# Summing the shift and scale parts of a modulation block in one tile, with other shares for VectorE and TensorE, and low parts of the first weights on GpSimd

## The chip, the cores and the metric

The kernel runs on one core of a Trainium2 chip. The metric is device time in microseconds of one execution, lower is better; the time before is the median of three runs, 2203.69 us (2201.57 to 2204.17). A core has TensorE (PE in the profile, its weight loads apart as PEld), VectorE (DVE), ScalarE (ACT), GpSimd (POOL) and queues for transfers, most of which SyncE (SP) issues here.

## The reference, cut to what the change touches

```python
c_act = jax.nn.silu(c)                            # c: (1, 1024)
mod = c_act @ w_mod[l] + b_mod[l]                 # w_mod: (1024, 3072)
shift, scale, gate = jnp.split(mod, 3, axis=-1)
h = rms_norm(x, g_norm[l]) * (1.0 + scale[:, None, :]) + shift[:, None, :]
proj = h @ w_in[l]                                # x: (1, 2048, 1024), w_in: (1024, 8192)
...
```

The projection feeds a recurrent branch and an attention branch, which are merged, projected and added to x. All of that lies behind the part in question. Here it matters that `h` needs shift and scale for each of its 1024 channels before the first product, and that each of these is a sum over 1024 terms `c_act[k] * w_mod[k, m]`.

## The kernel before, in words

Channels are laid on the 128 partitions, so 1024 channels are eight groups k (`KT = 8`, `KH = 4` is half of them). The first bank of 512 positions is built group by group: four transposes on TensorE turn x into channels by positions (`turn_x`, L688, to `turned`, L554), ScalarE makes the high part of h from PSUM with gain `gs` and bias `sh` (L564) and once more the full value `hf` (L567), and VectorE subtracts the two for the low part (L168). High and low parts let TensorE multiply in a reduced format three times and add (`mm3`): 12 multiplications of 512 columns a group (`products(k)`, four outputs of three). Their other operand, the first eight rows of tiles of the value weights (`raws`), is split in the same way by `split_k`: high part on ScalarE (L159), low part by `lo_dve` on VectorE (L168).

Shift and scale come in four blocks j of 256 channels, that is, two groups each. Tile `w_m[j, q]` holds all eight k of block j for shift (q = 0) or scale (q = 1), 1 MB, loaded by SyncE (L649). A block's sum over k is shared between two engines. `KV[j][q]` says how many k VectorE takes (`sums`): the first with one instruction of 256 elements (L658), each further one with a multiply-add on an accumulator (L661). TensorE takes the others (`column_sums`): for each k two multiplications with one column, the weights as the stationary operand and `ca[:, k]` as the moving one, into a PSUM tile V. Then `last_sums` folds VectorE's accumulators over the partitions, by the same kind of multiplication with a column of ones, and `modulation` (L684, L685) adds the bias and makes the gain on VectorE. In the profile a one-column multiplication leaves two records each of a weight load and a multiplication.

`idle_matmuls` issues multiplications of 512 columns on constants (tile `busy`), whose results nobody reads; here they are called fillers. `column_sums(0, 0, fill=1)` puts one behind every second k.

All this stands inside `manual_schedule()`: each engine runs its instructions in the order of the program's text. From the loop over j on, the order is: last sums of block j, its modulation, the rest of the products of group 2j - 1, turn of group 2j + 1, build and products of group 2j, VectorE's terms of block j + 1, with build 2j + 1 among them, splits of the next weights, turn of group 2j + 2, column sums of block j + 1 and the first half of the products of group 2j + 1. So the modulation of block j + 1 comes behind all of VectorE's terms and TensorE's columns for it. Behind this part (from L802 on) a planner orders the instructions up to the attention, which has an order of its own.

x itself is normalised first: ScalarE sums squares of its four tiles of rows (L715), VectorE finishes the factor (L172 to L181) and scales rows 0, 1 and 3 (L718), ScalarE row 2 (L734).

Of the kernel before, what the change touches and what calls it, by code (L numbers as in the profile page):

```python
# [20 lines left out]
P = 128  # L21
# [21 lines left out]
KV = (0, 3), (4, 3), (6, 5), (6, 5)  # L43
# [47 lines left out]
def decoder_block(ctx, tc, x, c, positions, g_norm, w_mod, b_mod, w_in, b_gate, conv_w, conv_b,  # L91
# [551 lines left out]
    w_m, px, accs = {}, {}, {}  # L643

    def load_mod(j):
        for q in range(2):
            w_m[j, q] = t = T(hp, [P, KT, 256], F32, "T", bufs=14)
            c0 = q * D + j * 256
            nc.sync.dma_start(t[:], w_mod[0, :, c0 : c0 + 256].rearrange("(k p) m -> p k m", p=P))  # L649

    def sums(j, q, ks=range(KT)):

        t = w_m[j, q]
        for k in ks[: KV[j][q] - ks[0]]:
            c = ca[:, k : k + 1]
            if k == 0:
                accs[j, q] = T(vx, [P, 256], F32, "acc", bufs=4)
                nc.vector.tensor_scalar(accs[j, q][:], t[:, k, :], c, None, ALU.mult)  # L658
            else:
                acc = accs[j, q]  # L660
                nc.vector.scalar_tensor_tensor(acc[:], t[:, k, :], c, acc[:], ALU.mult, ALU.add)  # L661

    def column_sums(j, q, fill=0):
        if q == 0:
            px["mod"] = T(pj, [P, 2, 2], F32, "V")
        pm, t = px["mod"], w_m.pop((j, q))
        for k in range(KV[j][q], KT):
            for i in range(2):
                mm(pm[:, q, i : i + 1], t[:, k, i * P : (i + 1) * P], ca[:, k : k + 1],
                   q == i == 0 and k == KV[j][0], q == i == 1 and (j, q) not in accs and k == KT - 1, skip_group_check=True)  # L670
            if fill and k % 2:
                idle_matmuls(fill)

    def last_sums(j, q):
        if (j, q) in accs:
            acc = accs.pop((j, q))
            for i in range(2):
                mm(px["mod"][:, q, i : i + 1], acc[:, i * P : (i + 1) * P], ones[:, 0:1],
                   False, q == i == 1, skip_group_check=True)
# [14 lines left out]
    with tc.manual_schedule():  # L694
# [21 lines left out]

        def scale_dve(r):
            nc.vector.tensor_scalar(x0[r], x0[r], norm[r // 2][:, 1, r % 2 : r % 2 + 1], None, ALU.mult)  # L718
# [11 lines left out]
        scale_dve(0)  # L730
        scale_dve(1)
        rstd_first(norm[1])
        rstd_last(norm[1])
        nc.scalar.activation(x0[2], x0[2], AF.Copy, scale=norm[1][:, 1, 0:1])  # L734
# [7 lines left out]
        def split_k(k):  # L742
            split_wide(ws[k // KH], k, raws.pop(k), lo_dve)
            n = k + NRAW
            if n < KT + KH:
                raws[n] = load_wide_raw(n // KT, n % KT)

        idle_matmuls(6)
        column_sums(0, 0, fill=1)
        idle_matmuls(2)  # L750
        sums(0, 1)
        column_sums(0, 1)
        split_k(0)
        idle_matmuls(2)
        last_sums(0, 1)
        modulation(0)
        turn_x(0)
        build_x(0)
        turn_x(1)
        idle_matmuls(2)  # L760
        split_k(1)
        pv0 = [pj_tile([P, CH]) for j in range(KH)]
        products(0)
        sums(1, 0)
        build_x(1)
# [5 lines left out]
        column_sums(1, 1)  # L771
        x1 = load_x(hp, 1, "T", 14)
        for j in range(1, 4):
            k = 2 * j
            for q in range(2):
                last_sums(j, q)
            modulation(j)
            products(k - 1, (2, 3))
            if j == 1:
                split_k(3)  # L780
# [3 lines left out]
            if j < 3:  # L784
                sums(j + 1, 0, range(3))
            build_x(k + 1)
            if j < 3:
                sums(j + 1, 0, range(3, KT))
                split_k(k + 2)
                turn_x(k + 2)  # L790
                column_sums(j + 1, 0)
                products(k + 1, (0, 1))
                sums(j + 1, 1)
                column_sums(j + 1, 1)
                split_k(k + 3)
# [1364 lines left out]
```

## Time and profile before

| | |
|---|---|
| median of three runs | 2203.69 us |
| the profiled execution | 2198.89 us |
| its span, first to last instruction | 2197.1 us |
| granted TensorE clock, mean over the span | 0.994 |
| the stretch up to 63 us: TensorE busy, granted clock | 58.73 us, 0.89 |
| the same: VectorE, ScalarE, GpSimd busy | 31.23, 26.47, 4.45 us |

Each row of a timeline has start and duration in us, engine, line, operation, tile written and tiles read with their sizes, the count of merged instructions and, in brackets, the engine's idle time before it and what ended it. In a row of windows each engine has its busy time and, in brackets, its count of instructions; then follow the granted TensorE clock (1.00 is full speed), the share of time that the 16 DMA engines were busy, and GB/s. In a row by line or tile, the three durations are the least, the median and the greatest in ns. Busy times of TensorE come from pipelined instructions that overlap, so the step from one to the next is shorter than the duration of one.

### The profile page before, as it was taken

How to read it: one execution, taken by the hardware profiler on the slowest of the kernel's cores; microseconds unless marked ns; L12 is line 12 of the kernel's file. 1: busy time of each engine (PE TensorE's matmuls, PEld its weight loads, DVE VectorE, ACT ScalarE, POOL GpSimd, SP SyncE). 2: the span in 40 equal slices, each digit the busy share in tenths (PEclk: the TensorE clock that was granted, in tenths of full speed). 3: DMA queues.
4: the chain of work that ended last, by engine and by line, in shares of the span. 5: the costliest groups of instructions: out<-in, count | busy, mean ns of one | idle time of the engine just before them, and what ended most of it. 6: DMA issues, size and time to landing. Idle time of an engine off the chain costs nothing.

```text
span 2197.1 us, 32892 instructions
## 1 busy us (share of the span) xinstructions
PE 2158.3 (98%) x10633; PEld 1804.7 (82%) x10634; DVE 1475.3 (67%) x2569; ACT 1311.0 (60%) x2619; POOL 1076.5 (49%) x804
## 2 busy tenths in 40 slices
PE   9999999999999999999999999999999999999998
PEld 7878888887788888888888887888888988877886
DVE  4748888867656715545447574566777777688887
ACT  3747678667644627457547522677888887434333
POOL 0457677766666423223224665465666665200443
PEclk8999999999999999999999999999999999999999
DMA  8367887886655378899996567877887786898552
GB/s 286 115 219 255 287 289 269 295 282 231 177 121 162 107 239 284 293 308 307 324 327 215 159 162 205 274 243 246 269 272 222 250 245 216 302 316 289 181 173 105
DMA packets 426480, 522.98 MB, mean 238 GB/s; under 512 B 104038, under 2 KB 291650, under 8 KB 425284
## 3 DMA queue, kind: packets, MB, share of 16 engines
q1 hardware_dynamic: 392164, 421.84, 61.8%
q10 hardware_dynamic: 33952, 98.99, 11.8%
q8 instruction: 84, 1.38, 0.2%
q14 instruction: 88, 0.72, 0.1%
q0 software_dynamic: 192, 0.05, 0.0%
HBM read 332.02 MB, written 188.75 MB: 237 GB/s over the span
## 4 chain that ended last, share of the span: by engine, by line
PE 55%; DMA 6%; DVE 3%; issue 3%; POOL 3%; ACT 2%; SPq 1%; ACTq 0%; POOLq 0%; DVEq 0%
PE X L151 11%; PE V L151 11%; PE pj L151 8%; PE Z L151 6%; PE W L151 6%; PE Y L151 5%; PE sc L151 3%; PE o L151 3%; PE pg L151 1%; POOL kq L165 1%; DMA S<-wD 1%; PE pT L1536 1%; PE pT L1549 1%; ACT pp L1452 1%; DMA kraw<-qT 1%
## 5 line engine op out<-in xcount | busy, mean ns | idle before, releaser
L165 POOL TENSOR_TENSOR S<-R,S 128x512 fp32r<-128x512 f32 x192 | 299.1, 1566 | 185.0 <-ACT S L159 105.5
L151 PE MATMUL pj<-yh,S 128*128 128x512 f32 x896 | 325.2, 404 | 3.3 <-DVE S L168 1.3
L151 PE MATMUL X<-T,S 128*128 128x512 f32 x1344 | 323.6, 390 | 2.7 <-ACT u L388 2.7
L151 PE MATMUL V<-T,S 128*128 128x512 f32 x1344 | 324.1, 390 | 0.2 <-DVE ev L458 0.2
L151 PEld LDWEIGHTS X<-T,S 128*128 128x128 f32 x1344 | 251.8, 188 | 56.5 <-ACT u L388 3.5
L151 PEld LDWEIGHTS V<-T,S 128*128 128x128 f32 x1344 | 252.0, 188 | 53.8 <-DVE ev L458 0.7
L165 POOL TENSOR_TENSOR S<-s,S 128x512 fp32r<-128x512 f32 x116 | 172.2, 1485 | 144.8 <-ACT S L159 107.9
L151 PEld LDWEIGHTS pj<-yh,S 128*128 128x128 f32 x896 | 168.4, 188 | 34.6 <-DVE S L168 2.2
L151 PE MATMUL pj<-yl,S 128*128 128x512 f32 x448 | 176.4, 394 | 3.1 <-DVE yl L168 2.0
L1452 ACT ACTIVATE pp<-pp,st 128x256 f32<-128x256 f32 (+3 forms) x256 | 133.5, 523 | 60.2 <-DVE st L1451 59.6
L151 PE MATMUL Z<-T,S 128*128 128x512 f32 x672 | 161.9, 390 | 0.0
L151 PE MATMUL Y<-T,S 128*128 128x512 f32 x672 | 161.8, 390 | 0.0
L151 PE MATMUL W<-T,S 128*128 128x512 f32 x672 | 161.6, 389 | 0.0
L159 ACT ACTIVATE S<-s 128x512 fp32r<-128x512 f32 x124 | 77.4, 624 | 131.9 <-DVE s L288 98.4
L159 ACT ACTIVATE S<-R 128x512 fp32r<-128x512 f32 x200 | 121.1, 621 | 51.4 <-DVE R L296 14.6
L168 DVE TENSOR_TENSOR ptl<-pT,pth 128x384 fp32r<-128x384 f32 (+1 forms) x160 | 97.9, 628 | 77.1 <-ACT pth L159 74.9
L151 PEld LDWEIGHTS W<-T,S 128*128 128x128 f32 x672 | 126.0, 188 | 26.9 <-issue 0.9
L151 PEld LDWEIGHTS Y<-T,S 128*128 128x128 f32 x672 | 125.9, 188 | 26.1
L151 PEld LDWEIGHTS Z<-T,S 128*128 128x128 f32 x672 | 125.8, 188 | 26.0
L942 DVE SCALAR_TENSOR_TENSOR xc<-xr,par,xc 128x512 f32<-128x512 f32 x96 | 103.3, 1076 | 55.9 <-ACT xc L936 53.7
L165 POOL TENSOR_TENSOR s<-R,s 128x512 fp32r<-128x512 f32 x32 | 43.7, 1367 | 190.7 <-ACT s L159 182.0
L1516 ACT ACTIVATE pp<-pp,M 128x256 f32<-128x256 f32 (+3 forms) x256 | 118.0, 523 | 9.7 <-DVE M L1639 9.7
(412 smaller groups left out, 4914.9 us busy)
## 6 DMA issues: line engine op xcount, KB each, us to landing
sD<-S ACTq DMA_DIRECT2D x140, 512.0 KB, 4.3
S<-sD SPq DMA_DIRECT2D x140, 512.0 KB, 5.2
S<-wD SPq DMA_DIRECT2D x82, 512.0 KB, 5.6
R<-in_w_in_dram SPq DMA_DIRECT2D x144, 256.0 KB, 4.2
wD<-s ACTq DMA_DIRECT2D x64, 256.0 KB, 4.7
T<-in_w_mod_dram SPq DMA_DIRECT2D x8, 1024.0 KB, 10.7
vN<-ev SPq DMA_DIRECT2D x32, 256.0 KB, 2.7
zaT<-ev SPq DMA_DIRECT2D x32, 256.0 KB, 3.6
```

Source lines behind the costliest of these rows:

```text
L151: nc.tensor.matmul(o, lhsT=l, rhs=r, start=st, stop=sp, **kw)
L159: nc.scalar.activation(o, i, AF.Copy)
L165: nc.gpsimd.tensor_tensor(o, i, h.bitcast(F32), ALU.subtract)
L168: return nc.vector.tensor_tensor(o, i, h.bitcast(F32), ALU.subtract).ins
L942: nc.vector.scalar_tensor_tensor(xc, xr[:, i : i + CH], cw(i), xc, ALU.mult, ALU.add)
L1452: nc.scalar.activation(pdst, pdst, AF.Exp, bias=m_, scale=-1.0, accum_out=l_)
L1516: nc.scalar.activation(pp, pp, AF.Copy, scale=w)
L1536: nc.tensor.transpose(pt[:, c0 + j * P : c0 + (j + 1) * P], pp[i][:, k * P : (k + 1) * P], ident)
L1549: nc.tensor.transpose(pt[:, c * P : (c + 1) * P], pp[:, half * P : (half + 1) * P], ident)
```

## The change

A tile of `w_mod` now holds one half kk of the k (four of them), with the shift and the scale columns of block j side by side, `[128, 4, 2, 256]`, loaded by two transfers of 512 KB. One VectorE instruction then sums 512 elements, shift and scale together, and there is one accumulator for a block. `KV[j][kk]` counts the k of each half that VectorE takes: 4, 6, 8 and 8 of the eight. TensorE's columns are left for two k of each half of block 0 and two of the second half of block 1; blocks 2 and 3 have none, and `starts` says which multiplication opens the sum in PSUM. `columns` does four one-column multiplications for a k or for the accumulator. `column_sums(j, 1)` now stands at the start of step j of the loop and no longer at the end of the step before.

The fillers are laid out anew: two behind each k of `column_sums(0, 0)`, one behind each of `column_sums(0, 1)`, one behind `last_sums(0)`; two behind `turn_x(1)` go. `split_k` makes the low part with the default `lo_pool` (GpSimd, L165) where it used `lo_dve`, and some splits stand elsewhere: `split_k(0)` ahead of the sums of (0, 1), and one split at the start of each step j. `turn_x(0)` moves ahead of `modulation(0)` in the text, `build_x(1)` ahead of `sums(1, 0)`. Row 0 of x is scaled on ScalarE, and the first terms of block 0 stand among the instructions that finish the norm.

```diff
--- before.py
+++ after.py
@@ -40,7 +40,7 @@
 TABLES = 24
 PIECES = (90, 94, 111, 116)
 
-KV = (0, 3), (4, 3), (6, 5), (6, 5)
+KV = (2, 2), (4, 2), (4, 4), (4, 4)
 
 
 C_C, C_G, C_BM, C_BG, C_CB, C_CW, C_BA, C_BX, C_LAM = 0, 8, 16, 40, 56, 64, 96, 104, 112
@@ -641,42 +641,44 @@
     gs = T(cp, [P, KT], F32, "gs")
     ca = T(cp, [P, KT], F32, "ca")
     w_m, px, accs = {}, {}, {}
+    starts = [next(((kk, kv[kk]) for kk in range(2) if kv[kk] < KH), None) for kv in KV]
 
     def load_mod(j):
-        for q in range(2):
-            w_m[j, q] = t = T(hp, [P, KT, 256], F32, "T", bufs=14)
-            c0 = q * D + j * 256
-            nc.sync.dma_start(t[:], w_mod[0, :, c0 : c0 + 256].rearrange("(k p) m -> p k m", p=P))
-
-    def sums(j, q, ks=range(KT)):
-
-        t = w_m[j, q]
-        for k in ks[: KV[j][q] - ks[0]]:
-            c = ca[:, k : k + 1]
-            if k == 0:
-                accs[j, q] = T(vx, [P, 256], F32, "acc", bufs=4)
-                nc.vector.tensor_scalar(accs[j, q][:], t[:, k, :], c, None, ALU.mult)
+        for kk in range(2):
+            w_m[j, kk] = t = T(hp, [P, KH, 2, 256], F32, "T", bufs=14)
+            for q in range(2):
+                c0 = q * D + j * 256
+                nc.sync.dma_start(t[:, :, q, :], w_mod[0, kk * KH * P : (kk + 1) * KH * P, c0 : c0 + 256].rearrange("(k p) m -> p k m", p=P))
+
+    def sums(j, kk, ks=range(KH)):
+
+        t = w_m[j, kk]
+        for k in ks[: KV[j][kk] - ks[0]]:
+            c = ca[:, kk * KH + k : kk * KH + k + 1]
+            if kk == k == 0:
+                accs[j] = T(vx, [P, 2, 256], F32, "acc", bufs=2)
+                nc.vector.tensor_scalar(accs[j][:], t[:, k], c, None, ALU.mult)
             else:
-                acc = accs[j, q]
-                nc.vector.scalar_tensor_tensor(acc[:], t[:, k, :], c, acc[:], ALU.mult, ALU.add)
-
-    def column_sums(j, q, fill=0):
-        if q == 0:
+                nc.vector.scalar_tensor_tensor(accs[j][:], t[:, k], c, accs[j][:], ALU.mult, ALU.add)
+
+    def columns(j, t, c, first, last, fill):
+        for i in range(4):
+            q, i = divmod(i, 2)
+            mm(px["mod"][:, q, i : i + 1], t[:, q, i * P : (i + 1) * P], c, first and q == i == 0, last and q == i == 1,
+               skip_group_check=True)
+        if fill:
+            idle_matmuls(fill)
+
+    def column_sums(j, kk, fill=0):
+
+        if kk == 0:
             px["mod"] = T(pj, [P, 2, 2], F32, "V")
-        pm, t = px["mod"], w_m.pop((j, q))
-        for k in range(KV[j][q], KT):
-            for i in range(2):
-                mm(pm[:, q, i : i + 1], t[:, k, i * P : (i + 1) * P], ca[:, k : k + 1],
-                   q == i == 0 and k == KV[j][0], q == i == 1 and (j, q) not in accs and k == KT - 1, skip_group_check=True)
-            if fill and k % 2:
-                idle_matmuls(fill)
-
-    def last_sums(j, q):
-        if (j, q) in accs:
-            acc = accs.pop((j, q))
-            for i in range(2):
-                mm(px["mod"][:, q, i : i + 1], acc[:, i * P : (i + 1) * P], ones[:, 0:1],
-                   False, q == i == 1, skip_group_check=True)
+        t = w_m.pop((j, kk))
+        for k in range(KV[j][kk], KH):
+            columns(j, t[:, k], ca[:, kk * KH + k : kk * KH + k + 1], (kk, k) == starts[j], False, fill)
+
+    def last_sums(j, fill=0):
+        columns(j, accs.pop(j), ones[:, 0:1], starts[j] is None, True, fill)
 
     def modulation(j):
         pm, j2 = px.pop("mod"), slice(2 * j, 2 * j + 2)
@@ -714,6 +716,9 @@
                 jk = T(vx, [P, D], BF16, "hf", bufs=2)
                 nc.scalar.activation(jk[:], x0[2 * i + n], AF.Square, accum_out=norm[i][:, 0, n : n + 1])
 
+        def scale_act(r):
+            nc.scalar.activation(x0[r], x0[r], AF.Copy, scale=norm[r // 2][:, 1, r % 2 : r % 2 + 1])
+
         def scale_dve(r):
             nc.vector.tensor_scalar(x0[r], x0[r], norm[r // 2][:, 1, r % 2 : r % 2 + 1], None, ALU.mult)
 
@@ -727,11 +732,13 @@
         nc.tensor.transpose(pt[:, :N_PAR], prow[:N_PAR, :], ident[:N_PAR, :N_PAR])
         nc.vector.tensor_copy(par[:], pt[:, :N_PAR])
         rstd_last(norm[0])
-        scale_dve(0)
         scale_dve(1)
+        sums(0, 0, range(1))
         rstd_first(norm[1])
+        scale_act(0)
+        sums(0, 0, range(1, KH))
         rstd_last(norm[1])
-        nc.scalar.activation(x0[2], x0[2], AF.Copy, scale=norm[1][:, 1, 0:1])
+        scale_act(2)
         scale_dve(3)
         ws = [wide_tiles() for kh in range(2)]
         even = ("B11", "B21")
@@ -740,59 +747,54 @@
             wide_products(pv0, even, ws[k // KH], (k,), js, first=k == 0, last=k == KT - 1)
 
         def split_k(k):
-            split_wide(ws[k // KH], k, raws.pop(k), lo_dve)
+            split_wide(ws[k // KH], k, raws.pop(k))
             n = k + NRAW
             if n < KT + KH:
                 raws[n] = load_wide_raw(n // KT, n % KT)
 
         idle_matmuls(6)
-        column_sums(0, 0, fill=1)
+        column_sums(0, 0, fill=2)
         idle_matmuls(2)
+        split_k(0)
         sums(0, 1)
-        column_sums(0, 1)
-        split_k(0)
+        column_sums(0, 1, fill=1)
         idle_matmuls(2)
-        last_sums(0, 1)
+        last_sums(0, fill=1)
+        turn_x(0)
         modulation(0)
-        turn_x(0)
         build_x(0)
         turn_x(1)
-        idle_matmuls(2)
         split_k(1)
         pv0 = [pj_tile([P, CH]) for j in range(KH)]
         products(0)
+        build_x(1)
         sums(1, 0)
-        build_x(1)
         split_k(2)
         turn_x(2)
         column_sums(1, 0)
         products(1, (0, 1))
         sums(1, 1)
-        column_sums(1, 1)
         x1 = load_x(hp, 1, "T", 14)
         for j in range(1, 4):
             k = 2 * j
-            for q in range(2):
-                last_sums(j, q)
+            column_sums(j, 1)
+            last_sums(j)
             modulation(j)
             products(k - 1, (2, 3))
-            if j == 1:
-                split_k(3)
+            split_k(k + 1)
             turn_x(k + 1)
             build_x(k)
             products(k)
             if j < 3:
-                sums(j + 1, 0, range(3))
+                sums(j + 1, 0, range(2))
             build_x(k + 1)
             if j < 3:
-                sums(j + 1, 0, range(3, KT))
+                sums(j + 1, 0, range(2, KH))
                 split_k(k + 2)
                 turn_x(k + 2)
                 column_sums(j + 1, 0)
                 products(k + 1, (0, 1))
                 sums(j + 1, 1)
-                column_sums(j + 1, 1)
-                split_k(k + 3)
         products(KT - 1)
         ws1 = wide_tiles()
         for k in range(KH):
```

## The prediction

> **What bounds the kernel now.** First I read the page's head, then the stretch that the change touches, from the loads to the end of the first eight products at 65.6 us, by windows cut where the granted clock changes. Columns: PE, PEld, DVE, ACT, POOL busy (instructions), PE clock, DMA share, GB/s.
>
> ```profile
> span 2197.1 us, 32892 instructions
> PE 2158.3 (98%) x10633; PEld 1804.7 (82%) x10634; DVE 1475.3 (67%) x2569; ACT 1311.0 (60%) x2619; POOL 1076.5 (49%) x804
> ...
> 5.20:15.40 10.20, 8.67 (x54) 5.38 (x52) 4.96 (x21) 7.21 (x13) 0.00 (x0) 1.00 1.06 369
> 15.50:25.70 10.20, 9.92 (x43) 8.62 (x44) 1.73 (x5) 1.63 (x3) 0.00 (x0) 0.50 1.09 355
> 25.70:35.90 10.20, 9.84 (x68) 8.62 (x66) 5.45 (x11) 3.34 (x6) 0.00 (x0) 1.00 1.10 352
> 36.00:39.30 3.30, 3.30 (x11) 2.61 (x11) 2.06 (x6) 1.45 (x2) 0.00 (x0) 0.50 1.08 420
> 49.60:59.80 10.20, 9.82 (x61) 8.34 (x60) 7.69 (x18) 3.80 (x7) 0.00 (x0) 1.00 0.17 51
> ```
>
> TensorE is busy nearly all the time here too, so a multiplication taken off it looks like time gained. Loads are not the bound: TensorE waited 0.6 us for `w_mod` in all (waits and DMA rows below). VectorE is 50 to 75% busy from 25.7 us on, GpSimd not at all. Next come the four blocks j of the modulation, in the timelines of VectorE, ScalarE and TensorE (start, duration):
>
> ```profile
> 23.74 0.16 DVE L684 TENSOR_TENSOR mod<-V,par 128x4 f32<-128x4 f32 x1 [6.79 <-PE V L151]
> ...
> 36.21 0.16 DVE L684 TENSOR_TENSOR mod<-V,par 128x4 f32<-128x4 f32 x1 [4.40 <-PE V L151]
> ...
> 47.26 0.16 DVE L684 TENSOR_TENSOR mod<-V,par 128x4 f32<-128x4 f32 x1 [0.42 <-PE V L151]
> ...
> 49.19 0.69 DVE L168 TENSOR_TENSOR T<-hf,T 128x512 fp32r<-128x512 f32 x1 [1.58 <-ACT hf L567]
> 49.80 0.35 DVE L658 TENSOR_SCALAR acc<-T,ca 128x256 f32<-128x256 f32 x1
> 50.18 1.00 DVE L661 SCALAR_TENSOR_TENSOR acc<-T,ca,acc 128x256 f32<-128x256 f32 x2
> 51.10 0.68 DVE L168 TENSOR_TENSOR T<-hf,T 128x512 fp32r<-128x512 f32 x1
> 51.70 1.52 DVE L661 SCALAR_TENSOR_TENSOR acc<-T,ca,acc 128x256 f32<-128x256 f32 x3
> 53.14 0.68 DVE L168 TENSOR_TENSOR S<-R,S 128x512 fp32r<-128x512 f32 x1
> ...
> 57.38 0.16 DVE L684 TENSOR_TENSOR mod<-V,par 128x4 f32<-128x4 f32 x1 [0.61 <-PE V L151]
> ```
> ```profile
> 14.15 1.15 ACT L734 ACTIVATE T<-T,ss 128x1024 f32<-128x1024 f32 x1 [1.02 <-DVE ss L181]
> ...
> 49.85 0.77 ACT L567 ACTIVATE hf<-pg,mod,gs 128x512 f32<-128x512 f32 x1
> 50.51 1.15 ACT L159 ACTIVATE S<-R 128x512 fp32r<-128x512 f32 x2
> ```
> ```profile
> 14.97 0.38 PE L151 MATMUL W<-busy 128*128 128x512 bf16 x1
> 15.18 1.43 PE L151 MATMUL V<-ca,T 128*128 128x1 f32 x8
> 16.47 1.23 PE L151 MATMUL W<-busy 128*128 128x512 bf16 x2
> 17.92 4.26 PE L151 MATMUL V<-ca,T 128*128 128x1 f32 x20 [0.22 <-issue]
> ...
> 46.19 1.03 PE L151 MATMUL V<-ones,acc 128*128 128x1 f32 x8
> ...
> 52.34 0.60 PE L554 MATMUL Y<-cs,T 128*128 128x128 f32 x4
> ...
> 64.77 0.84 PE L151 MATMUL X<-S,T 128*128 128x512 f32 x3
> ```
>
> The modulations start at 23.74, 36.21, 47.26 and 57.38, so a block's cycle takes 12.47, 11.05 and 10.12 us. VectorE's wait just before the last two (0.42, 0.61 us) shows that its chain of sums ends almost with TensorE's column sums: the two engines are **level** there, and relief for TensorE alone is worth little.
>
> **The change part by part.**
>
> *TensorE's columns.* A column multiplication leaves two records; a record takes 1.03/8 with its end, 0.11 us in a row, and 4.26/20 = 0.21 us at half clock. Before there are 128 records of columns and 28 of last sums. After: (0,0), (0,1) and (1,1) have two k each, 8 records a k, 48; last sums 4 x 8 = 32. So 76 records fewer, 76 x 0.112 = 8.5 us of TensorE at full clock. That is the gain if TensorE stayed the bound.
>
> *Sums on VectorE.* Prices:
>
> ```profile
> L942 DVE SCALAR_TENSOR_TENSOR xc<-xr,par,xc x96: 739/753/1855, 155.2 to 1195.8; 128x512 f32<-128x512 f32 x96
> ...
> L658 DVE TENSOR_SCALAR acc<-T,ca x7: 346/347/352, 14.9 to 53.7; 128x256 f32<-128x256 f32 x7
> L718 DVE TENSOR_SCALAR T<-T,ss x3: 748/752/753, 11.4 to 14.1; 128x1024 f32<-128x1024 f32 x3
> ...
> 155.16 4.46 DVE L942 SCALAR_TENSOR_TENSOR xc<-xr,par,xc 128x512 f32<-128x512 f32 x3 [2.74 <-ACT xc L936]
> ...
> 156.18 1.75 POOL L165 TENSOR_TENSOR S<-s,S 128x512 fp32r<-128x512 f32 x1
> 157.89 1.19 POOL L165 TENSOR_TENSOR gl<-ev,gh 128x256 fp32r<-128x256 f32 x1
> ...
> L165 POOL TENSOR_TENSOR S<-R,S x192: 1278/1305/5445, 62.1 to 1335.2; 128x512 fp32r<-128x512 f32 x192
> ```
>
> A term of 512 costs 0.753 (the same operation and size at L942), with 0.03 between dependent ones 0.785; the first term (TENSOR_SCALAR of 512) lies a third of the way from 0.347 to 0.752, so 0.48, taken as 0.50. Before: 7 first terms x 0.38 + 25 x 0.515 = 15.5 us. After: 4 x 0.50 + 22 x 0.785 = 19.3 us. Eight low parts leave VectorE, 8 x 0.60 = 4.8 us. So VectorE's own work falls by about 1 us; it is the order that costs.
>
> *Low parts on GpSimd.* Each takes 1.28 us there and has no queue ahead of it. But the rows at 155 us show the two engines in each other's way: three dependent L942 terms take 4.46 us where 3 x 0.785 = 2.36 was due, 2.1 more beside two GpSimd subtractions (which themselves stretch to 1.75), so about **1.0 us a meeting**; the slowest L942, 1.855, is 1.1 over the median. Where do they meet? ScalarE makes two high parts of S right behind the odd `hf` (50.51), and each releases a low part, just when VectorE begins its longest run of dependent sums. With two meetings in each of three cycles that is 6.0 us. Bounds: 0 if all fall in VectorE's wait for `hf` (1.58 us a cycle), 6 x 1.28 = 7.7 if each stops it for the whole subtraction; I take 1.0, the measured meeting. The Trainium skill (SBUF — State Buffer, "SBUF: two separate sides") says the pair of ports is an exclusive lock for a whole instruction when VectorE reads two SBUF inputs; by it the term would be 7.7 and the sum 1.7 us later. The rows show somewhat less.
>
> *Up to the first modulation.* TensorE starts at 12.04 with the first tile. After: 8 records 0.88, two fillers 0.44 (0.22 each), 8 records 0.88, four fillers 0.87: 15.1. If the clock halves at 15.47 as before: 13 more column records at 0.21, four fillers at 0.43, 8 last records and the hand-over of 0.2 come to 22.1, a gain of 1.65. At full clock to there (16 x 0.11 + 4 x 0.22 + 1.03 + 0.1): 18.9, a gain of 4.85. VectorE's four terms end near 17, behind the second tile (first used at 14.92), so they aren't late. Which clock? Busy time of the wide multiplications alone (fillers, then products, then products again):
>
> ```profile
> 5.20:15.40 10.20, 6.22 (x25) 2.44 (x23) 0.00 (x0) 1.00 1.06 369
> ...
> 25.70:35.90 10.20, 5.02 (x18) 3.23 (x18) 1.37 (x2) 1.78 (x3) 0.00 (x0) 1.00 1.10 352
> ...
> 49.60:59.80 10.20, 6.55 (x25) 4.21 (x24) 1.37 (x2) 1.44 (x3) 0.00 (x0) 1.00 0.17 51
> ```
>
> After the first of these (61% wide) the clock halved, after the second too (5.02 + 0.60 for a turn, 55%); after the third (6.55 + two turns of 0.60, 76%) it didn't. Columns, though they keep TensorE busy, seem to count for little. The changed kernel has three fillers more before 15.47, so 6.9 us, 67%: between, and I take the middle, **-3.25**.
>
> *The cycles.* VectorE's chain from one modulation to the next: to the even low part 1.93 (47.26 to 49.19, through ScalarE's two builds), that part 0.61, first term 0.50, one term 0.785, odd low part 0.61, six terms 4.71, two meetings 2.0, last sums and the hand-over 1.07 (46.19 to 47.26): **12.2**. TensorE has 1.03 + 24 x 0.228 (0.84 less its end for three) + 2 x 0.43 = 7.4 us of work in it and waits. Against 11.05 and 10.12 that is **+1.15** and **+2.1**. For j = 0 to 1 ScalarE's chain leads (0.45, four builds and one high part 3.33), then 0.61 + 0.50 + 5 x 0.785 + 2.0 + 1.07: 11.9, against 12.47: **-0.6**. After the fourth modulation nothing changes.
>
> *Clock in the cycles.* 24 products and two turns in 12.2 us are about 7.3 of wide work, 60%, as much as where it halved. A halving of 3.3 us as at 36.0 mostly falls into TensorE's new idle time; on the path it lengthens last sums by 0.9 and turns with products by 1.1. Bounds 0 and 2 x 2.0 + 1.7 for the last products, 5.7. I take **+1.5**.
>
> *At nothing.* The scaling of row 0 on ScalarE (L734, 1.15 us) ends near 14.3, turned after 18.9; uncovered, 1.15. Sixteen issues of half the size move the same bytes in the same 1 KB rows; these are the rows:
>
> ```profile
> PE V L151 <- DMA T<-in_w_mod_dram: 0.6, 1, 0.6
> ...
> L649 SPq DMA_DIRECT2D T<-in_w_mod_dram x8: 432/1582/3097, 1.6 to 25.6; - x8
> ```
>
> SP's queue already paces itself on the transfers (3.1 an issue, 1.06 DMA share), so the second half could cost one issue, 0.43, at 12.04, and later blocks have slack.
>
> Sum: -3.25 - 0.6 + 1.15 + 2.1 + 1.5 = **+0.9 us**. The profiled execution took 2198.89 us (span 2197.1 and 1.8 around it), so 2199.8; the median of the runs is 4.8 above it, 2203.69, so **2204.6**.
>
> **The rivals.** *GpSimd misses the chain* (faster): the cycles lose 6.0 and the sum is -5.1: 2198.6. For it: 1.58 us of VectorE idle in each cycle and an idle GpSimd. Against: the place of the high parts at 50.51.
>
> *The clock stays low* (slower): VectorE's chain leaves TensorE a gap of about 6.71 - 1.4 = 5.3 us a cycle, wide work is 60%, and each cycle pays the full 2.0, the last products 1.7, and the first stretch halves as now (-1.65): -1.65 - 0.6 + 1.15 + 2.1 + 5.7 = +6.7: 2210.4. It decides once a stretch falls under some 61%. The Trainium skill (TensorE: Matmul & The Clock Gate, "Why this matters for your kernels") asks for no idle gap over about 3 us between bursts; by it every cycle would halve the clock, this rival's time. The trace says that idleness is not needed: it halved at 15.5 with no TensorE gap over 1 us shown here.
>
> *The order behind it shifts*: what follows is laid out by a planner, not by hand.
>
> ```profile
> 63.00:600.00 537.00, 531.37 (x2357) 437.30 (x2356) 410.82 (x489) 369.03 (x602) 360.90 (x241) 1.00 0.72 245
> ```
>
> TensorE is idle there for 5.6 us. Another order could win that at most, or lose as much: 2199.0 or 2210.2. Nothing in the profile favours either.
>
> *The change doesn't do what it says*: GpSimd is starved and products wait for low parts. One subtraction did take 5.445, but beside independent VectorE work; dependent sums leave gaps. Worth +4 at one such stall: 2208.6.
>
> **How the numbers follow.** Forecast 0.48; GpSimd misses the chain 0.17; clock low 0.20; another order 0.12 (0.05 faster, 0.07 slower); starved 0.03. A measurement of this kernel tells about 0.2%, 4.4 us, from no change. Faster 0.17 + 0.05 = 0.22, slower 0.20 + 0.07 + 0.03 = 0.30, same 0.48. The extremes of the bounds are -8.3 (full clock early, no meetings, no halving: -4.85 - 0.6 + 1.15 + 2.1 - 6.0) and +8.4 (clock low with meetings of 1.28). The range 2198 to 2211.5 leaves out about 0.2.
>
> **What would show it.** Modulations near 20, 32, 44 and 57 us, VectorE's L661 at 0.75 alone and 1.7 beside a GpSimd L165, TensorE idle 4 to 5 us before each last sum from j = 2 on, the clock at 1.00 through 15.5. Cycles of 10.2 us would mean no meetings; modulations spaced as now but all earlier would mean that TensorE, not VectorE, still leads. I am wrong if the time lies beyond 4.4 us of 2203.69.

## The result and the profile after

| | before | after |
|---|---|---|
| median, 12 runs each, in turn on one chip | 2203.39 us (2199.90 to 2206.21) | 2207.15 us (2204.53 to 2209.68) |
| the profiled execution | 2198.89 us | 2206.91 us |
| fourth modulation starts, in the profiled execution | 57.38 us | 59.76 us |
| first eight products end, in the profiled execution | 65.61 us | 68.94 us |

The ratio is 1.0018, with a 95% interval of 1.0010 to 1.0027: 3.8 us more, clear of nothing (the interval is some 2.2 to 5.9 us) and itself less than the 4.4 us that were named as the bound. The two profiled executions lie 8.0 us apart, since that of before was 4.5 us quicker than its own median; totals are therefore compared by medians, and only the stretch that the change touches by profiles. In these two executions that stretch became 3.3 us longer, which is nearly the whole.

The head of the page of the kernel after, with one row of the operations of one line: VectorE's L944 is the L942 of before, the first such term long behind the stretch.

```profile
span 2205.1 us, 32752 instructions
PE 2158.8 (98%) x10558; PEld 1801.1 (82%) x10559; DVE 1484.8 (67%) x2554; ACT 1312.3 (60%) x2620; POOL 1090.7 (49%) x812
...
L944 DVE SCALAR_TENSOR_TENSOR xc<-xr,par,xc x96: 740/752/1855, 160.1 to 1201.2; 128x512 f32<-128x512 f32 x96
```

TensorE has 75 records of multiplications fewer and yet is busy half a microsecond longer: the columns went, and the time came back. The first L944 comes 4.9 us later than in before, the last one 5.4: what was lost was lost early and not made up. 3.3 of the 4.9 lie in the stretch; the other 1.6 are about what one later fall of the clock would cost (0.50 at 121.2, in the last section).

VectorE's timeline of the kernel after, from the first modulation to the fourth (L686, L684 before; L660 and L662 are L658 and L661 before):

```profile
18.68 0.16 DVE L686 TENSOR_TENSOR mod<-V,par 128x4 f32<-128x4 f32 x1 [1.87 <-PE V L151]
...
23.79 0.48 DVE L660 TENSOR_SCALAR acc<-T,ca 128x512 f32<-128x512 f32 x1
24.30 5.75 DVE L662 SCALAR_TENSOR_TENSOR acc<-T,ca,acc 128x512 f32<-128x512 f32 x5
32.00 0.16 DVE L686 TENSOR_TENSOR mod<-V,par 128x4 f32<-128x4 f32 x1 [1.96 <-PE V L151]
...
35.06 0.75 DVE L662 SCALAR_TENSOR_TENSOR acc<-T,ca,acc 128x512 f32<-128x512 f32 x1
37.11 0.69 DVE L168 TENSOR_TENSOR T<-hf,T 128x512 fp32r<-128x512 f32 x1 [1.29 <-ACT hf L567]
37.72 6.63 DVE L662 SCALAR_TENSOR_TENSOR acc<-T,ca,acc 128x512 f32<-128x512 f32 x6
46.37 0.16 DVE L686 TENSOR_TENSOR mod<-V,par 128x4 f32<-128x4 f32 x1 [2.02 <-PE V L151]
...
51.87 6.68 DVE L662 SCALAR_TENSOR_TENSOR acc<-T,ca,acc 128x512 f32<-128x512 f32 x6
59.76 0.16 DVE L686 TENSOR_TENSOR mod<-V,par 128x4 f32<-128x4 f32 x1 [1.21 <-PE V L151]
```

GpSimd's timeline beside it, and TensorE's last sums and the end of the eight products:

```profile
37.67 2.98 POOL L165 TENSOR_TENSOR S<-R,S 128x512 fp32r<-128x512 f32 x2 [9.74 <-ACT S L159]
```
```profile
30.10 1.86 PE L151 MATMUL V<-ones,acc 128*128 128x1 f32 x8 [1.97 <-DVE acc L662]
...
44.49 1.84 PE L151 MATMUL V<-ones,acc 128*128 128x1 f32 x8 [4.17 <-DVE acc L662]
...
58.70 1.02 PE L151 MATMUL V<-ones,acc 128*128 128x1 f32 x8 [4.35 <-DVE acc L662]
...
68.10 0.84 PE L151 MATMUL X<-S,T 128*128 128x512 f32 x3
```

Three things are to be seen. VectorE's terms of 512 cost 0.753 alone, but six in a row take 6.63 and 6.68 us where 4.71 was due: the two low parts on GpSimd begin within 0.05 us of that chain, at 37.67 (and again at 51.88). TensorE waits 4.2 and 4.4 us for the chain. And the last sums behind two of the three waits take 1.85 us, not 1.02: the clock was at half. Windows cut at the clock's changes:

```profile
22.10:28.90 6.80, 6.04 (x36) 5.23 (x36) 5.58 (x6) 2.31 (x4) 4.05 (x3) 1.00 1.08 352
28.90:35.70 6.80, 5.60 (x19) 4.91 (x20) 3.17 (x7) 1.52 (x3) 0.00 (x0) 0.50 1.10 352
35.80:42.50 6.70, 4.52 (x22) 3.38 (x20) 5.30 (x6) 2.43 (x4) 2.96 (x2) 1.00 1.04 413
42.60:49.30 6.70, 4.81 (x16) 4.15 (x17) 3.01 (x7) 1.45 (x2) 0.00 (x0) 0.50 0.33 124
49.40:59.60 10.20, 5.85 (x34) 4.70 (x32) 7.87 (x8) 2.48 (x4) 2.98 (x2) 1.00 0.18 52
59.70:63.00 3.30, 3.30 (x12) 2.61 (x11) 1.02 (x3) 2.08 (x3) 0.00 (x0) 0.50 0.02 5
```

Each stretch at full clock with a wait in it is followed by one at half: three times, and the half clock meets the last sums, the first products behind the modulation and the turns, which lie on the chain to the next modulation. A fourth fall, at 18.7, has no such wait ahead of it.

### The profile page after: what moved, and what is told of

It is laid out like the page before. It is cut to its first block, busy times and chain, and to the rows that moved or that the text cites. A ratio compares the mean times of both kernels' runs of the same rounds, so it can differ in the third digit from the quotient of the medians.

```text
span 2205.1 us, 32752 instructions
## 1 busy us (share of the span) xinstructions
PE 2158.8 (98%) x10558; PEld 1801.1 (82%) x10559; DVE 1484.8 (67%) x2554; ACT 1312.3 (60%) x2620; POOL 1090.7 (49%) x812
## 4 chain that ended last, share of the span: by engine, by line
PE 60%; DMA 5%; DVE 3%; issue 2%; POOL 2%; ACT 2%; SPq 1%; ACTq 0%; POOLq 0%; DVEq 0%
PE X L151 12%; PE V L151 11%; PE pj L151 10%; PE Z L151 6%; PE W L151 6%; PE Y L151 5%; PE sc L151 3%; PE o L151 3%; PE pg L151 1%; PE pT L1538 1%; PE pT L1551 1%; DMA kraw<-qT 1%; DMA S<-wD 1%; POOL q L1415 1%; POOL kq L165 1%
## 5 line engine op out<-in xcount | busy, mean ns | idle before, releaser
L165 POOL TENSOR_TENSOR S<-R,S 128x512 fp32r<-128x512 f32 x200 | 313.0, 1573 | 176.5 <-ACT S L159 84.3
L165 POOL TENSOR_TENSOR S<-s,S 128x512 fp32r<-128x512 f32 x116 | 172.0, 1483 | 145.1 <-ACT S L159 106.2
L944 DVE SCALAR_TENSOR_TENSOR xc<-xr,par,xc 128x512 f32<-128x512 f32 x96 | 102.6, 1069 | 59.2 <-ACT xc L938 56.9
L165 POOL TENSOR_TENSOR s<-R,s 128x512 fp32r<-128x512 f32 x32 | 43.6, 1362 | 191.1 <-ACT s L159 169.0
```

Of the source, the lines that this page charges most:

```text
L165: nc.gpsimd.tensor_tensor(o, i, h.bitcast(F32), ALU.subtract)
L944: nc.vector.scalar_tensor_tensor(xc, xr[:, i : i + CH], cw(i), xc, ALU.mult, ALU.add)
```

## The experiments

Two theories of the loss stood against each other. **Meetings:** VectorE and GpSimd are in each other's way during the chain of sums. **Clock:** TensorE's waits for that chain let the clock fall, and the fall lengthens what lies on the chain. E1 to E4, E5 to E8, and E9 and E10 were timed in three series, each on one chip in turn with before (medians of before: 2203.31, 2203.11, 2203.63); the first row is the result above. The fourth modulation is that of each one's profiled execution.

| kernel | fourth modulation, us | median, us | ratio to before, 95% interval |
|---|---|---|---|
| the changed one | 59.76 | 2207.15 | 1.0018, 1.0010 to 1.0027 |
| E1 low parts on VectorE | 54.32 | 2198.05 | 0.9980, 0.9972 to 0.9989 |
| E2 fillers in the waits | 55.74 | 2202.62 | 0.9995, 0.9985 to 1.0006 |
| E3 before, with low parts on GpSimd | 59.28 | 2204.72 | 1.0011, 1.0000 to 1.0021 |
| E4 two k back to TensorE | 57.65 | 2204.07 | 1.0003, 0.9994 to 1.0013 |
| E5 low parts in VectorE's wait, fillers | 54.50 | 2197.10 | 0.9973, 0.9964 to 0.9982 |
| E6 as E5, three k of the second half | 49.98 | 2198.04 | 0.9981, 0.9971 to 0.9991 |
| E7 fewer fillers in block 0 | 58.38 | 2205.74 | 1.0017, 1.0007 to 1.0027 |
| E8 as E1, with fillers | 53.23 | 2199.05 | 0.9981, 0.9972 to 0.9990 |
| E9 as E6, without fillers | 49.28 | 2198.43 | 0.9977, 0.9968 to 0.9986 |
| E10 as E5, fewer fillers | 50.09 | 2198.31 | 0.9978, 0.9966 to 0.9990 |

**E1: the meetings taken away.** The changed kernel, with the first weights' low parts on VectorE, in the same places of the text.

```diff
-            split_wide(ws[k // KH], k, raws.pop(k))
+            split_wide(ws[k // KH], k, raws.pop(k), lo_dve)
```

> The changed kernel with the eight low parts of the first weights back on VectorE, at the same places of the text. In the profile of the changed kernel GpSimd's low parts lengthen VectorE's runs of sums by about 1.9 us in each of three cycles. Theory 'meetings': one low part a cycle (0.6 us) then stands in VectorE's run and the other in its wait for hf, so a cycle gets 1.3 us shorter, 4 us in all: near 2203. Theory 'clock' alone (the cycles are long because the TensorE clock is halved in them): no change beyond 1 us, near 2207. Both at work: near 2203, with the clock still halved two or three times before 65 us.

VectorE's timeline between the second and the third modulation, then windows at and behind the waits, of E1:

```profile
35.38 1.53 DVE L662 SCALAR_TENSOR_TENSOR acc<-T,ca,acc 128x512 f32<-128x512 f32 x2
36.83 0.68 DVE L168 TENSOR_TENSOR S<-R,S 128x512 fp32r<-128x512 f32 x1
37.43 3.10 DVE L662 SCALAR_TENSOR_TENSOR acc<-T,ca,acc 128x512 f32<-128x512 f32 x4
```
```profile
34.20:41.00 6.80, 4.46 (x23) 3.41 (x23) 5.62 (x8) 1.68 (x3) 0.00 (x0) 1.00 1.07 399
41.00:47.80 6.80, 6.80 (x23) 5.63 (x23) 3.22 (x7) 3.38 (x6) 0.00 (x0) 0.50 0.58 217
```

The six terms and the low part among them take 5.15 us (35.38 to 40.53) where the six alone took 6.63: a low part costs VectorE 0.60 when it makes it, and 0.96 when GpSimd does. The clock still falls in this kernel, at 30.8, 41.0 and 54.7. The median is 9.1 us below that of the changed kernel, more than the 4 us expected. Of these the fourth modulation shows 5.4 us; for the other 3.7 the profiled executions offer only that E1's had two falls of the clock between 100 us and the end of the work, the changed kernel's five. Whether that belongs to the kernels or to the executions isn't settled.

**E2: the waits filled.** The meetings stay; 6, 18 and 18 fillers that nobody reads are issued ahead of the columns and last sums of blocks 1, 2 and 3.

```diff
+GAP = (0, 6, 18, 18)
...
-        if kk == 0:
+        if kk == (j > 0):
+            if j:
+                tv = T(pj, [P, CH], F32, "V")
+                for _ in range(GAP[j]):
+                    mm(tv[:], busy[:, :P], busy[:], True, True)
```

> The changed kernel with fillers (6, 18 and 18 wide multiplications on constants, 0.22 us each at full clock) in TensorE's gap ahead of the column sums and last sums of blocks 1, 2 and 3; low parts stay on GpSimd. Theory 'clock': the clock stays at 1.00 from about 22 us on, last sums take 1.0 in place of 1.85 us, the odd hf no longer waits for its turn (1.29 and 1.09), the last products aren't halved (1.0): 5 us in all, near 2202. Theory 'meetings' alone: VectorE's chain is as long as before, near 2207; the fillers lie in idle time and cost nothing.

Windows, VectorE's and TensorE's timelines of E2:

```profile
31.40:34.70 3.30, 3.30 (x12) 2.63 (x11) 1.86 (x4) 2.47 (x5) 0.00 (x0) 0.50 1.11 349
34.80:45.00 10.20, 10.09 (x52) 6.63 (x52) 7.26 (x9) 1.97 (x4) 2.83 (x2) 1.00 1.01 388
45.10:55.30 10.20, 9.72 (x49) 6.07 (x48) 8.80 (x10) 2.87 (x5) 3.22 (x2) 1.00 0.19 55
```
```profile
35.29 6.62 DVE L663 SCALAR_TENSOR_TENSOR acc<-T,ca,acc 128x512 f32<-128x512 f32 x6
```
```profile
38.39 4.06 PE L152 MATMUL V<-busy 128*128 128x512 bf16 x17
42.51 1.05 PE L152 MATMUL V<-ones,acc 128*128 128x1 f32 x8
```

The six terms take 6.62 as before: nothing changed on VectorE or GpSimd. The fillers stand where TensorE waited, the clock stays at 1.00 from 34.8 on, the last sums take 1.05, and the time falls by 4.5 us, as expected. So work that computes nothing made the kernel faster, by most of what the clock had cost. The cycles are 11.98, 13.12 and 12.15 us; the prediction had 11.9, 12.2 and 12.2 ahead of its clock term, and the one cycle that is longer holds the one stretch at half clock that is left. Of its extra 0.9 us, 0.4 are VectorE's wait for an `hf` in that stretch; the fillers, which end some 0.5 us behind the sums (41.91), account for the rest. The first cycle owes less to the fillers: in this execution the clock didn't fall at 18.7, ahead of the first of them.

**E3: low parts on GpSimd, and nothing else.** The kernel before with that one edit.

```diff
-            split_wide(ws[k // KH], k, raws.pop(k), lo_dve)
+            split_wide(ws[k // KH], k, raws.pop(k))
```

> The kernel before, with nothing but the eight low parts of the first weights moved to GpSimd. There VectorE's run of sums ends level with TensorE's columns (it waits 0.4 to 0.6 us for the last sums). Theory 'meetings': each cycle gets 2 x (1.0 - 0.6) less that wait longer, 0.3 to 0.8 us, 1 to 2 us in all: 2204.5 to 2205.5, with L661 terms of about 1.4 us beside GpSimd. If GpSimd's low parts come for nothing: VectorE saves 1.2 us a cycle, TensorE leads, 2203.4 or a little less.

Three terms of 256 beside two low parts, on VectorE's and GpSimd's timelines of E3:

```profile
52.73 3.51 DVE L661 SCALAR_TENSOR_TENSOR acc<-T,ca,acc 128x256 f32<-128x256 f32 x3
```
```profile
52.74 2.70 POOL L165 TENSOR_TENSOR S<-R,S 128x512 fp32r<-128x512 f32 x2 [9.46 <-issue]
```

In before the same three terms took 1.52: two meetings cost 1.99, so the price doesn't hang on the size of the terms. The median came out inside the 2204.5 to 2205.5 expected. This part alone makes the kernel some 1.4 us slower, with an interval from 0 to 4.6 us.

**E4: shares back to TensorE.** Two k of the second half of blocks 1, 2 and 3 return from VectorE to TensorE's columns, in the changed kernel.

```diff
-KV = (2, 2), (4, 2), (4, 4), (4, 4)
+KV = (2, 2), (4, 0), (4, 2), (4, 2)
```

> The changed kernel with VectorE's share of blocks 1, 2 and 3 cut from 6, 8 and 8 of the eight k to 4, 6 and 6; the rest are TensorE columns (0.9 us a k). Theory 'chain' (VectorE's run sets the cycle): 2 x 0.785 us less in each run, TensorE's extra 1.8 us lie in its gap of 4.2 us for blocks 2 and 3 and about replace the gap for block 1: 1.6 + 1.6 + 0.2, near 2203.8. If TensorE's work or the clock alone set the cycle: up to 5.4 us slower, 2208 to 2212.

3.1 us below the changed kernel, as expected: in the second and third cycle (12.55 and 12.66 us for 14.37 and 13.39) VectorE's chain was the longer one, and a shorter one is worth time although TensorE gets 8 column records for every k. The first cycle became longer instead, 13.91 for 13.32: there VectorE waited 4.0 us for TensorE.

**E7: the start.** Five of the fillers in block 0 taken out of the changed kernel again.

```diff
-        column_sums(0, 0, fill=2)
+        column_sums(0, 0, fill=1)
-        column_sums(0, 1, fill=1)
+        column_sums(0, 1)
-        last_sums(0, fill=1)
+        last_sums(0)
```

> The changed kernel with five fillers fewer in block 0 (one behind each k of the first tile, none behind those of the second, none behind the last sums). Theory 'fillers hold the clock to 18.7 us': it halves near 15.5 us again, as in the kernel before, and the first modulation comes at about 21 instead of 18.7 us, though 1.1 us of fillers are gone; time up to 2.5 us more, 2207 to 2209.5, less where the later halvings fall better. If the clock does not hang on them: first modulation near 18.2, time 0.5 less.

VectorE's first modulation of E7 and the two windows about it:

```profile
18.59 0.16 DVE L686 TENSOR_TENSOR mod<-V,par 128x4 f32<-128x4 f32 x1 [2.07 <-PE V L151]
```
```profile
6.30:16.50 10.20, 9.46 (x59) 6.08 (x57) 6.36 (x22) 8.72 (x15) 0.21 (x1) 1.00 1.07 363
16.60:26.80 10.20, 10.01 (x33) 7.78 (x32) 4.83 (x8) 4.57 (x7) 4.09 (x4) 0.50 1.10 354
```

A miss for the first theory. The first modulation came at 18.59, as early as in the changed kernel, and the ratio is the changed kernel's. The half clock did come, for 10.2 us, but at 16.6, behind the columns of block 0. It lengthened the last sums from 0.95 to 1.71 us, less than the five missing fillers saved (5 x 0.22), and what followed of it didn't show in the time. The fillers that the change adds in block 0 earn nothing that shows here.

**E5, E6, E8, E9, E10: a version that beats both.** E1 and E2 each gain, and low parts can also go where VectorE waits for `hf`. E5 does both: low parts by `lo_dve`, two of them right behind each modulation, and 2, 12 and 12 fillers by E2's lines.

```diff
-        split_k(0)
         sums(0, 1)
+        split_k(0)
...
-        split_k(2)
...
             modulation(j)
+            split_k(k)
+            split_k(k + 1)
             products(k - 1, (2, 3))
-            split_k(k + 1)
...
-                split_k(k + 2)
```

> Low parts on VectorE, those of two groups right behind each modulation, where VectorE waits 1.6 us for hf; fillers (2, 12, 12) in TensorE's gap ahead of the sums of blocks 1 to 3; VectorE's shares as in the changed kernel. Theory 'meetings and clock' (both costs are real, and nothing else sets the cycle): no meetings, clock at 1.00 from 20 us on, cycles of 9.9, 10.2 and 10.2 us, first modulation at 18.7, the eight products done near 57 us instead of 68.9: 10 to 11 us less than the changed kernel, near 2196.5, and 1.5 to 4 less than with low parts on VectorE alone. If VectorE's run had another bound (loads, ScalarE): no better than with low parts on VectorE alone, 2198.

VectorE's timeline of E5 behind the second modulation:

```profile
32.85 0.16 DVE L691 TENSOR_TENSOR mod<-V,par 128x4 f32<-128x4 f32 x1 [1.68 <-PE V L152]
...
33.12 1.29 DVE L169 TENSOR_TENSOR S<-R,S 128x512 fp32r<-128x512 f32 x2
...
37.18 4.68 DVE L663 SCALAR_TENSOR_TENSOR acc<-T,ca,acc 128x512 f32<-128x512 f32 x6
```

The two low parts take 1.29 of a wait that was 1.57 in the changed kernel, the six terms their 4.68, and the clock stays at 1.00 from 25 us on. At 2197.1 it is the quickest median of all, 6.0 us below before and 10 below the changed kernel. It lies near the 2196.5 expected, but not by the expected way: in the profiled execution the first modulation came at 21.50 for 18.7, the cycles took 11.35, 10.83 and 10.82 us for 9.9, 10.2 and 10.2, and the eight products ended at 62.7 for 57. E8 is E1 with E2's lines and 2, 10 and 10 fillers; E6 is E5 with `KV` of (4, 3) for blocks 2 and 3 and 2, 6 and 6 fillers.

> The changed kernel with the low parts back on VectorE at the same places, and fillers (2, 10, 10) in TensorE's gap ahead of the sums of blocks 1 to 3. Theory 'meetings and clock': cycles of about 10.8 us with the clock at 1.00, products done near 60.5 us: 2 to 3 us less than with low parts on VectorE alone (2198.05), near 2195.5. If the clock's halvings there fell into TensorE's idle time: 2198.

> As the kernel with the low parts in VectorE's wait, but VectorE takes 7 of the eight k of blocks 2 and 3, TensorE one (0.9 us), fillers 2, 6, 6. Theory 'chain': VectorE's run is 0.785 shorter in two cycles, TensorE has room: 1.6 us less again, cycles of 9.4 us. If TensorE leads by then: no change against that kernel.

E8's second and third cycle were 10.70 and 10.69 us, and E6's 10.45 and 10.43; E6's should have been 9.4, and its fillers made TensorE the later engine (VectorE waited 2.2 us for it). Both medians stayed at E1's, 3 us or more above what was expected; so beside low parts on VectorE the fillers of E8 earned nothing that shows. E9 takes all of E6's fillers out, E10 brings E5's down to 0, 8 and 8.

> The kernel with the low parts in VectorE's wait and KV (4,3) for blocks 2 and 3, with no fillers in the gaps. Theory that the fillers led there and that wide work alone now fills enough of a 10 us stretch: cycles of 1 to 3 of about 9.4 us instead of 10.45, granted clock 1.00 from 30 us to 60 us, eight products ended 2 to 3 us earlier, near 56 us, and a median of 2194 to 2196. Rival (what follows the products swallows what is gained ahead of them): cycles as short, but a median at 2197 to 2199, as with the four versions before. Rival (the fillers are what holds the clock): a half-clock stretch inside 30 to 60 us and cycles of 10.5 us or more.

> Low parts in VectorE's wait, shares of the changed kernel, fillers 0, 8 and 8 instead of 2, 12 and 12. Theory that twelve fillers ended 0.6 us after VectorE's sums: cycles 2 and 3 near 10.2 us instead of 10.8, clock 1.00 there, and a median 1 to 2 below 2197.1: 2195 to 2196. Rival (the order behind the products and the clock in each execution set what is left): median 2197 to 2199 all the same.

TensorE's timeline of E9 at the last two modulations, and windows of it:

```profile
38.83 1.05 PE L152 MATMUL V<-ones,acc 128*128 128x1 f32 x8 [0.72 <-DVE acc L663]
...
48.19 1.05 PE L152 MATMUL V<-ones,acc 128*128 128x1 f32 x8 [0.42 <-DVE acc L663]
```
```profile
29.00:32.40 3.40, 3.40 (x12) 2.71 (x12) 2.62 (x6) 1.45 (x2) 0.00 (x0) 0.50 1.09 354
32.50:42.70 10.20, 9.17 (x54) 7.56 (x53) 7.45 (x13) 4.89 (x8) 0.00 (x0) 1.00 1.05 390
...
49.50:52.90 3.40, 3.40 (x12) 2.72 (x11) 2.04 (x4) 1.75 (x3) 0.00 (x0) 0.50 0.45 134
```

E9's third cycle is 9.36 us, the 9.4 expected; the second was 10.54 with half clock in its start, and the clock fell again at 49.5 although TensorE had waited no more than 0.72 us. E10's cycles are 10.99, with half clock at 29.8, and 10.21. Both medians are the rival's, 2197 to 2199; E9's second cycle and its half clock at 49.5 are also what its other rival named, that the fillers hold the clock. So six versions whose fourth modulation lies anywhere from 49.3 to 54.5 us end within 2 us of each other, and their intervals overlap. In single executions the gain is still there far behind the stretch:

```profile
L944 DVE SCALAR_TENSOR_TENSOR xc<-xr,par,xc x96: 745/752/1862, 154.6 to 1195.5; 128x512 f32<-128x512 f32 x96
```
```profile
L948 DVE SCALAR_TENSOR_TENSOR xc<-xr,par,xc x96: 740/753/1859, 148.9 to 1189.5; 128x512 f32<-128x512 f32 x96
```

The first row is E1's, the second E6's: 5.7 us apart at the first such term and 6.0 at the last, but only 2.6 at the end of the spans (2196.3 and 2193.7), and nothing in the medians. Of what takes it behind 1195 us the traces show one piece: E6's clock was at half at 1898.5 and at 1987.2, E1's at 1990 alone. Whether more falls there follow from an earlier front or belong to the execution isn't shown, and stays open.

## Why the prediction came out as it did

The sign of the forecast, +0.9 us, was right, and the time lies inside the range; 2.9 us of the 3.8 were missed. In the profiled executions two misses of opposite sign partly cancel, the start (1.8 us better than taken) and the clock in the cycles (4.2 worse), and that is luck. By its steps:

| step | taken, us | measured, us |
|---|---|---|
| to the first modulation | -3.25 | -5.06 (18.68 for 23.74) |
| first cycle | -0.6 | +0.85 (13.32 for 12.47) |
| second cycle | +1.15 | +3.32 (14.37 for 11.05) |
| third cycle | +2.1 | +3.27 (13.39 for 10.12) |
| behind the fourth modulation | 0 | +0.95 (9.18 for 8.23) |
| clock in the cycles, apart | +1.5 | 5.7, contained in the four rows above |
| sum | +0.9 | +3.3 |

**The step that failed**, a term with the wrong size, is "Clock in the cycles": "a halving of 3.3 us as at 36.0 mostly falls into TensorE's new idle time". The last four rows of steps exceed the prediction's by 1.42 (13.32 against 11.9), 2.17, 1.19 and 0.95, together 5.7. That is the upper bound that stood beside the term. The fall doesn't spend itself in the wait: it began 0.8 us into the wait of 2.0, 2.2 us into the one of 4.2 and 0.9 us behind the one of 4.4, and outlasted each. At 42.6 it began 1.9 us ahead of the last sums and lasted 6.8, over the last sums (+0.8), the products behind them and the turn, until the odd `hf` came 1.1 us late. Some 0.5 us of the 5.7 belong to the fall at 18.7, behind no such wait: the first low part comes 2.64 us behind the modulation there, 2.16 in E2. E2 shows the cause of most of the rest: with the waits filled the time falls by 4.5 us, and its third cycle, at full clock throughout, took 12.15 us, the prediction's 12.2.

**Meetings** were 6.0 us in the prediction and are 5.7: 1.83 (5.75 for five terms, 3.93 due), 1.92 and 1.97. Place and price were right, the price with some luck: the 2.1 us read at 155 us fell beside three GpSimd instructions, not two (L922, from 154.93 to 156.23, is the third). The prediction weighed the Trainium skill's rule of the lock here (SBUF — State Buffer, "SBUF: two separate sides"): where VectorE has two inputs in SBUF and GpSimd reads SBUF too, whoever starts first has the shared ports for the whole instruction. It took that to mean 1.28 us a meeting and found the rows to show less. The single instructions of the second cycle, VectorE's and GpSimd's, agree with the rule better than that:

```profile
37.72 1.79 DVE L662 SCALAR_TENSOR_TENSOR acc<-T,ca,acc 128x512 f32<-128x512 f32 x1
...
39.54 1.65 DVE L662 SCALAR_TENSOR_TENSOR acc<-T,ca,acc 128x512 f32<-128x512 f32 x1
```
```profile
37.67 1.29 POOL L165 TENSOR_TENSOR S<-R,S 128x512 fp32r<-128x512 f32 x1 [9.74 <-ACT S L159]
...
38.98 1.67 POOL L165 TENSOR_TENSOR S<-R,S 128x512 fp32r<-128x512 f32 x1
```

The two take turns. Each term ends some 0.55 us behind the low part beside it (39.51 for 38.96, 41.19 for 40.65), though it takes 0.753 alone; the second low part ends 1.14 behind the first term, though it takes 1.28 alone. So each seems to wait for the other's end with all but its first 0.1 to 0.2 us, and a meeting costs VectorE 0.96 and not 1.28 because that beginning passes during the wait.

**Prices**: a term 0.753, the first term 0.48, TensorE's waits 4 to 5 us from the second cycle on, all as worked out.

**The start** gained 5.06 in this execution, not 3.25: the clock stayed at 1.00 to 18.7. The two bounds were 1.65 at half clock and 4.85 at full, and the middle was taken. (The sum at half clock, of 13 column records, four fillers, 8 last records and the hand-over, 15.47 + 2.73 + 1.72 + 1.68 + 0.2, comes to 21.8 and not 22.1, a gain of 1.9.) Which of the two it is differs from execution to execution: E5, E6, E9 and E10 have the same instructions up to there, the changed kernel's but for the first low part, and their first modulations came at 21.50, 18.41, 18.68 and 18.70; the clock fell at 14.7 in E5 and not before the modulation in the others. How often the changed kernel's clock falls early isn't known from one profile, so what the start is worth in its median stays open.

**The rivals.** "The clock stays low" is what happened in the cycles, with the start at full clock: -4.85 - 0.6 + 1.15 + 2.1 + 5.7 = +3.5, against 3.3 measured. Its condition, "it decides once a stretch falls under some 61%", doesn't hold up (last section). "GpSimd misses the chain" fell at the first timeline; E1, which takes the meetings away by another way, shows that they were worth the 6.0 us of the forecast and more: 9.1 us by the medians. "The order behind it shifts" is neither shown nor excluded: the lag of 4.9 us at the first L944 is 5.4 at the last. "GpSimd is starved" didn't come: each of its low parts up to 55 us took less than 1.8 us.

The Trainium skill's rule on the clock (TensorE: Matmul & The Clock Gate, "Why this matters for your kernels"), that idle gaps over some 3 us bring it down, agrees with the changed kernel's waits of 4.2 and 4.4 us, which both met a fall, though the first one came after 2.2 us of the wait. E1's clock fell at 41.0 behind a wait of 2.3 us and E9's at 49.5 with none over 0.72, so short waits are no protection here.

## What to carry to other kernels

Where one engine is relieved and starts to wait for another, price the wait twice: its length, and the clock that falls behind it and meets the next thing on the chain; useless multiplications in the wait won 4.5 us here (E2), though nothing that shows once the meetings were gone (E8). A small piece of work moved to an idle engine isn't free if it is released at the moment when the busy engine begins its longest dependent run: 1.28 us of GpSimd cost VectorE 0.96, more than the 0.60 of doing it itself, while the same piece in VectorE's own wait cost nothing that shows. A gain ahead of a long rest must be read from the medians, since up to 6 us that were plain in the traces at 150 us were not in the end. And one profile shows one execution: with the same instructions, E5's first modulation came 3 us later than E6's.

## What the runs showed of the hardware

The clock changed to 0.50 and back in steps of 3.4, 6.8 or 10.2 us, and its place differs also where two kernels begin almost alike: the first fall came at 15.5 us (before), 18.7 (after), 14.7 (E5) and 16.6 (E7). No share of wide multiplications in the 10.2 us ahead decides it. Four such windows, the busy time of the fillers alone (tile `busy`), of after, E5, E7 and once more after:

```profile
5.00:15.20 10.20, 6.75 (x28) 2.50 (x26) 0.00 (x0) 1.00 1.06 370
```
```profile
4.40:14.60 10.20, 6.97 (x30) 2.70 (x28) 0.00 (x0) 1.00 1.06 372
```
```profile
6.30:16.50 10.20, 6.09 (x25) 2.29 (x23) 0.00 (x0) 1.00 1.07 363
```
```profile
8.40:18.60 10.20, 5.25 (x20) 2.06 (x19) 0.00 (x0) 1.00 1.09 354
```

Behind the first nothing fell (66% wide); behind the second the clock fell for 10.2 us with 68%, behind the third for 10.2 with 60%, behind the fourth for 3.4 with 51%. So the 61% of the prediction was no threshold, and what sets the length of a fall isn't found.

The falls of one execution stand on a grid: in all twelve traces they begin whole multiples of 3.413 us apart (after: 18.67, 28.91, 42.56, 59.63 and 121.07, which are 3, 4, 5 and 18 steps). The grid lies differently to the first instruction in each execution, so the same wait is cut by it in another place each time. That fits the four first modulations above, and where in a wait a fall begins.

Falls also come late, where TensorE is otherwise busy. These windows of the kernel after are the step ahead of the fall at 121.07 and the fall:

```profile
117.60:121.00 3.40, 1.45 (x7) 0.89 (x6) 3.33 (x3) 1.56 (x3) 2.60 (x2) 1.00 0.00 0
...
121.20:124.40 3.20, 3.08 (x8) 1.97 (x7) 2.09 (x4) 2.73 (x5) 0.00 (x0) 0.50 0.85 233
```

TensorE was idle for 1.95 us of the step ahead. The other late falls are like it: between 100 us and the last 25 us the twelve traces hold 22 falls, each behind a step with 1.2 to 2.0 us of idle TensorE. Of the 100 steps of the grid there that had 1.0 us or more of it at full clock, 22 were followed by a fall, of the 7156 with less none. The early falls need no idleness: at 15.5 (before) TensorE had been busy for the whole step ahead, with one-column multiplications among the rest.

A step of 3.4 us at half speed delays a busy TensorE by 1.7 us, and the profiled executions here had between none (E4, E5) and five of them behind 100 us. The spread of single runs, some 5 to 12 us in each kernel, goes by and large with the clock: of the 33 runs of before in the second series the quickest, 2198.69 us, had a mean granted clock of 0.996, the slowest, 2206.78, one of 0.992. That is a reason to compare medians.
